# The later modulation units of a mixer-and-FFN kernel, put behind other weight tiles and in another order

## The chip, the cores and the metric

The kernel runs on one core of one Trainium2 chip. The metric is the device time of one execution in microseconds. All data are fp32; a product that has to be exact to fp32 is made of three passes over a rounded high part and a remainder ("hi" and "lo") of each operand.

## The reference

One block of a transformer with adaptive modulation, on 256 tokens of width 1024:

```
mod = silu(c) @ w_ada + b_ada                  # 6 rows of 1024: sh1 sc1 g1 sh2 sc2 g2
h   = x * (1 + sc1) + sh1
y   = token_mixer(h)                           # attention, retention, two gated projections, w_out
x   = layer_norm(ALPHA * x + g1 * y, ln1_g, ln1_b)
h   = x * (1 + sc2) + sh2
y   = conv_ffn(h)                              # gate and up, a convolution of 3 tokens, gelu, down
x   = layer_norm(ALPHA * x + g2 * y, ln2_g, ln2_b)
```

Each row of `mod` is a product of a 1024 x 1024 part of `w_ada` with one vector. It is not made on TensorE: a unit of the weights is loaded with the output index on the partitions, and VectorE multiplies it with the vector and sums along the row.

## The kernel before

**Stages.** A first stage (`h1`, `x_prod`, `halve`) makes the first two modulation rows, h, and the first part of the input projection. Then comes a list of `main` weight tiles, each 128 x 2048 floats (1 MB), in a fixed order: tiles 0 and 1 for the retention keys, 2 to 5 its values, 6 to 9 its gate, 10 to 15 the two merge gates, 16 and 17 the moba projection (`wpm`), 18 to 21 the retention projection (`wpr`), 22 to 25 `w_out`, 26 and 27 the first up block, and from 28 on the gate, up and down tiles of the FFN. Up to tile 23 a tile is used in two steps, one for each half: step s uses half s. `LN1_AT` = 48 is the first step of tiles 24 and 25.

**The way of a tile.** `load_next` (L1237) takes the next entry of `stream` and starts its DMA on the SyncE queue (`load_raw`, L102) into one of `RAW_BUFS` = 4 raw buffers. The buffers go round, so a load waits until the entry four places ahead in the stream has been read for the last time. `prep_halves` (L1242) takes the loaded tiles half by half. For each half, ScalarE rounds it (`whi`, L1263), always one half ahead, and then VectorE makes the remainder (`wlo`, L1277). After the second half the raw buffer is free and the next load is asked for. TensorE uses both in `mm3` (L115 to L117), three matmuls for each product.

**The later modulation rows.** The rows 2 (scale) and 3 (shift) of the second half of the block and the two gates, 4 and 5, each come in four units of 1 MB (`ada_unit`, L952). A unit is put into `stream` behind a weight tile. When `prep_halves` meets one, it puts its two halves on `chain` and goes on with the next weight tile; after each further half of a weight tile it takes one entry off the chain:

```python
    chain.append((raw, half, fn))                # raw_halves, on meeting a unit
    ...
    if chain:                                    # behind each half's wlo
        raw, k, fn = chain.pop(0)
        fn(raw, k, S["main"])                    # one reduction, L227
        if k == 1:
            load_next()
```

So a unit behind tile m has its two reductions behind halves 2m+1 and 2m+2, and its raw buffer is held until then. After the last unit of a row, L957 adds the bias. For the gates `rows_done` (L961) then writes the row of 1024 to DRAM and reads it back as a broadcast to all partitions (L965, L966), both on the GpSimd queue: 4 KB and 0.5 MB. The first gate's broadcast goes to the buffer R0, which the rotated retention operands had before; it is read in L564, after step 47. Scale and shift are read in `out_start` (L702 to L704), after step 48.

**What sets the order.** The engines' programs are written out by the loop over steps (L1312). In step s, `prep_to` prepares halves up to s + 1 + 4 for steps under 22 and up to s + 1 + 6 from there to step 46. Three times a step a piece of the side work is put in between: attention, retention, the transposes, all of it spread over VectorE, ScalarE and TensorE. At the end of a step that completes a product stand the instructions that empty its banks: L518 (ScalarE, the merge gate, after steps 27 and 31), L525 (VectorE, after steps 33 and 35), L544 and L545 (VectorE, after steps 39 and 43). The products take banks 0, 1 and 2, 3 in turn, so the product of steps 34 and 35 uses the banks that L518 empties after step 31, steps 36 to 39 those of the first L525, and so on. Before steps 42 and 45 the merged result is transposed on TensorE (L536) and split (L92, L93). Each engine works through its own program in order; an instruction that waits holds up all that stand behind it on its engine.

The functions that the diff touches, and what calls them:

Of the kernel before, what the change touches and what calls it, by code (L numbers as in the profile page):

```python
# [46 lines left out]
def mixer_ffn(tc, a, out):  # L47
    nc = tc.nc
    pe, act, dve, sp = nc.tensor, nc.scalar, nc.vector, nc.sync
    cst = tc.tile_pool(name="cst", bufs=1)  # L50
    pools = [cst, tc.tile_pool(name="wts", bufs=1), tc.tile_pool(name="big", bufs=1),
             tc.tile_pool(name="tmp", bufs=2),
             tc.tile_pool(name="ps", bufs=1, space=bass.MemoryType.PSUM),
             tc.tile_pool(name="dram", bufs=1, space=bass.MemoryType.DRAM)]
    with tc.manual_schedule():
        with pools[0] as cst, pools[1] as wts, pools[2] as big, pools[3] as tmp, pools[4] as ps, \
                pools[5] as dram:
            _body(nc, a, out, pe, act, dve, sp, cst, wts, big, tmp, ps, dram)


def _body(nc, a, out, pe, act, dve, sp, cst, wts, big, tmp, ps, dram):
# [890 lines left out]
    def ada_unit(secs, u, done):  # L952

        def fn(raw, k, step):
            ada(raw[:, k * 1024:(k + 1) * 1024], secs, 2 * u + k)
            if u == 3 and k == 1:
                dve.tensor_tensor(mod[:, secs], mod[:, secs], bcol[:, secs], OP.add)  # L957
                later.append((step + 7, done))
        return fn

    def rows_done(sec):  # L961

        g = S["g", sec - 4] = slot(f"R{sec - 4}", [128, 1024])
        row = dram.tile([1, 1024], F32, name=f"row{sec}")
        nc.gpsimd.dma_start(row.rearrange("o (p j) -> (o p) j", p=128), mod[:, sec])  # L965
        nc.gpsimd.dma_start(g, row.to_broadcast([128, 1024]))  # L966
# [256 lines left out]


    extra = {}
    for sec, at in ((2, (9, 10, 11, 12)), (3, (13, 14, 15, 16)), (4, (17, 18, 19, 20)), (5, (38, 41, 44, 47))):
        for u in range(4):
            done = (lambda sec=sec: rows_done(sec)) if sec > 3 else (lambda: None)
            extra.setdefault(at[u], []).append((a["ada2"][sec - 2, u], ada_unit(sec, u, done)))
# [204 lines left out]
```

## Time and profile before

| | |
|---|---|
| time, median of 3 runs | 431.37 us (430.92 to 431.76) |
| profiled execution | 431.65 us, span 429.9 us |
| busy: TensorE, VectorE, ScalarE | 416.4, 370.8, 246.0 us |
| DMA | 105.58 MB, mean 246 GB/s |
| the modulation reductions, L227, from 128 x 1024 | 32 (with the first stage's), 38.9 us |
| loads of units (`in_ada`) | 16 of 1 MB |

Busy times overlap; the matmuls are pipelined, so their single durations add up to more than the time they take. A row of the timeline gives the start in us, the duration, the engine and the line, the operation, output and inputs, and in brackets the idle time of the engine ahead of it and what ended that. `AH`, `AYa` and the like are buffers, `P` is a bank of PSUM, `raw`, `whi` and `wlo` are the three forms of a weight tile.

### The profile page before, as it was taken

Reading aid. Unit: us, or ns where it says so; the run is one execution under the profiler, and the core shown is the slowest. Engines: PE = TensorE matmul, PEld = TensorE weight load, DVE = VectorE, ACT = ScalarE, POOL = GpSimd, SP = SyncE. Lnnn points to the kernel's source line nnn. Section 1 sums busy time; section 2 is a strip of 40 time slices with the busy share of each in tenths; the row PEclk is TensorE's granted clock in tenths of the full one; section 3 lists DMA queues with packets and bytes.
Section 4 is the critical chain, followed back from the end, with each engine's and each line's share of the span. In section 5 each row is a group of like instructions: output and inputs, shape, how many; then the busy total and the mean of one; then the engine's idle time right before and its main releaser. Section 6 shows DMA issues by size and latency. Waiting matters only on the chain.

```text
span 429.9 us, 5794 instructions
## 1 busy us (share of the span) xinstructions
PE 416.4 (97%) x2104; PEld 349.6 (81%) x2104; DVE 370.8 (86%) x613; ACT 246.0 (57%) x397; POOL 14.0 (3%) x26
## 2 busy tenths in 40 slices
PE   8999999999999999699999999999999999999993
PEld 4888888887888887578888899888888888888882
DVE  5979899768969989899878897899999888789976
ACT  4666567688953647355433894664555555455700
POOL 0000000100000000000000000100000000002200
PEclk9999999999999999979999999999999999999998
DMA  8998996754387698989953066885875777450001
GB/s 284 408 409 330 418 417 248 285 179 186 110 304 263 217 355 305 348 348 311 386 191 139 2 240 250 311 290 194 307 274 208 287 292 247 185 196 2 1 24 73
DMA packets 18828, 105.58 MB, mean 246 GB/s; under 512 B 2288, under 2 KB 3568, under 8 KB 8048
## 3 DMA queue, kind: packets, MB, share of 16 engines
q1 hardware_dynamic: 17280, 99.97, 62.1%
q0 software_dynamic: 1376, 4.99, 3.4%
q8 instruction: 16, 0.26, 0.2%
q10 hardware_dynamic: 144, 0.26, 0.2%
q14 instruction: 12, 0.10, 0.1%
HBM read 104.15 MB, written 1.06 MB: 245 GB/s over the span
## 4 chain that ended last, share of the span: by engine, by line
PE 87%; DVE 8%; DMA 3%; issue 1%; ACT 0%; DVEq 0%; ACTq 0%; SPq 0%
PE P L124 15%; PE P L115 14%; PE P L116 14%; PE P L117 14%; PE P L301 13%; PE P L126 8%; DVE junk L227 2%; DVE wlo L1277 2%; DMA raw<-in_wpm 2%; DMA raw<-in_wpr 2%; PE P L688 1%; PE P L690 1%; PE P L691 1%; PE P L993 1%; PE P L1048 1%
## 5 line engine op out<-in xcount | busy, mean ns | idle before, releaser
L1277 DVE TENSOR_TENSOR wlo<-raw,whi 128x1024 fp32r<-128x1024 f32 x118 | 142.0, 1218 | 17.0 <-ACT whi L1263 17.0
L1263 ACT ACTIVATE whi<-raw 128x1024 fp32r<-128x1024 f32 x118 | 122.0, 1055 | 48.5 <-PE P L117 14.4
L115 PE MATMUL P<-whi,AH 128*128 128x512 f32 x160 | 63.4, 397 | 0.0
L117 PE MATMUL P<-whi,AH 128*128 128x512 f32 x160 | 62.3, 390 | 0.0
L116 PE MATMUL P<-wlo,AH 128*128 128x512 f32 x160 | 62.3, 389 | 0.0
L301 PE MATMUL P<-whi,AH 128*128 128x512 f32 x160 | 42.0, 392 | 0.0
L227 DVE CUSTOM_DVE_ANT_0 junk<-raw,srow 128x1024 bf16<-128x1024 f32 x32 | 38.9, 1217 | 0.5 <-DMA raw<-in_ada 0.5
L124 PE MATMUL P<-AYa,whi 128*128 128x512 f32 x144 | 39.2, 393 | 0.0
L124 PE MATMUL P<-AYb,whi 128*128 128x512 f32 x144 | 38.6, 390 | 0.0
L301 PEld LDWEIGHTS P<-whi,AH 128*128 128x128 f32 x160 | 29.8, 188 | 7.2 <-ACT whi L284 0.8
L115 PEld LDWEIGHTS P<-whi,AH 128*128 128x128 f32 x160 | 30.0, 188 | 6.8 <-issue 0.7
L117 PEld LDWEIGHTS P<-whi,AH 128*128 128x128 f32 x160 | 30.0, 188 | 6.4
L116 PEld LDWEIGHTS P<-wlo,AH 128*128 128x128 f32 x160 | 30.1, 188 | 5.9
L465 ACT ACTIVATE A<-P 128x256 f32<-128x256 f32 x36 | 13.7, 381 | 34.5 <-PE P L126 32.6
L124 PEld LDWEIGHTS P<-AYb,whi 128*128 128x128 f32 x144 | 27.0, 188 | 6.0
L284 ACT ACTIVATE whi<-raw 128x512 fp32r<-128x512 f32 (+1 forms) x26 | 20.8, 824 | 17.8 <-DMA raw<-in_strm 16.2
L287 DVE TENSOR_TENSOR wlo<-raw,whi 128x512 fp32r<-128x512 f32 (+1 forms) x26 | 23.7, 936 | 6.0 <-ACT whi L284 5.8
L124 PEld LDWEIGHTS P<-AYa,whi 128*128 128x128 f32 x144 | 25.1, 190 | 3.6
L126 PEld LDWEIGHTS P<-AYa,wlo 128*128 128x128 f32 x144 | 22.0, 189 | 2.8
L301 PE MATMUL P<-wlo,AH 128*128 128x512 f32 x80 | 23.3, 391 | 0.0
L126 PE MATMUL P<-AYb,wlo 128*128 128x256 f32 x144 | 23.1, 283 | 0.0
L126 PE MATMUL P<-AYa,wlo 128*128 128x256 f32 x144 | 22.9, 282 | 0.0
(302 smaller groups left out, 739.3 us busy)
## 6 DMA issues: line engine op xcount, KB each, us to landing
raw<-in_ada SPq DMA_DIRECT2D x16, 1024.0 KB, 4.9
raw<-in_wup SPq DMA_DIRECT2D x11, 1024.0 KB, 4.9
raw<-in_wgate SPq DMA_DIRECT2D x11, 1024.0 KB, 5.5
raw<-in_wdown SPq DMA_DIRECT2D x11, 1024.0 KB, 5.2
raw<-in_winB SPq DMA_DIRECT2D x10, 1024.0 KB, 6.3
raw<-in_strm SPq DMA_DIRECT2D x8, 1024.0 KB, 7.8
raw<-in_strm SPq DMA_DIRECT2D x12, 512.0 KB, 7.4
raw<-in_winGr SPq DMA_DIRECT2D x4, 1024.0 KB, 6.1
```

The source lines that it names most:

```text
L115: pe.matmul(o, lh, rh, start=start, stop=False)
L116: pe.matmul(o, lh, rl, start=False, stop=False)
L117: pe.matmul(o, ll, rh, start=False, stop=stop)
L124: pe.matmul(o, wh[:, k * 128:(k + 1) * 128], x2[k], start=k == 0, stop=False)
L126: pe.matmul(o[:, :256], wl[:, k * 128:(k + 1) * 128], x2[k][:, 0], start=False, stop=k == n - 1)
L227: dve.tensor_tensor_reduce(out=nobody(j if own else None), in0=raw, in1=srow, scale=1.0, scalar=0.0, op0=OP.mult, op1=OP.add, accum_out=mo ...
L284: act.activation(hi[:, o], raw[:, o], AF.Copy)
L287: dve.tensor_tensor(lo[:, o], raw[:, o], f(hi[:, o]), OP.subtract)
L301: pe.matmul(pa[b0 + c // 512 * 2 + t], x[xi][:, j, t * 128:(t + 1) * 128], ws[k][:, c:c + 512], start=first and (xi, k) == (0, 0), stop=la ...
L465: act.activation(t, p[:, 256:], AF.Copy)
L1263: act.activation(hi, src, AF.Copy)
L1277: dve.tensor_tensor(lo, src, f(hi), OP.subtract)
```

## The change

The table that says behind which weight tiles the units of each row stand is altered: the first gate's units come first, then scale, then shift, and the twelve units that stood behind the twelve tiles 9 to 20 now stand behind tiles of 8 to 22, with none behind 10, 15 and 19. The units of row 5 stay. Nothing else is touched.

```diff
-    for sec, at in ((2, (9, 10, 11, 12)), (3, (13, 14, 15, 16)), (4, (17, 18, 19, 20)), (5, (38, 41, 44, 47))):
+    for sec, at in ((4, (8, 9, 11, 12)), (2, (13, 14, 16, 17)), (3, (18, 20, 21, 22)), (5, (38, 41, 44, 47))):
         for u in range(4):
             done = (lambda sec=sec: rows_done(sec)) if sec > 3 else (lambda: None)
             extra.setdefault(at[u], []).append((a["ada2"][sec - 2, u], ada_unit(sec, u, done)))
```

## Prediction

> **What bounds the kernel now.** I read the page first, then the waits of TensorE, then the stage around its one large wait.
>
> ```profile
> span 429.9 us, 5794 instructions
> PE 416.4 (97%) x2104; PEld 349.6 (81%) x2104; DVE 370.8 (86%) x613; ACT 246.0 (57%) x397; POOL 14.0 (3%) x26
> ...
> raw<-in_ada SPq DMA_DIRECT2D x16, 1024.0 KB, 4.9
> ```
>
> TensorE is busy 416.4 of 429.9 us, so a change that leaves the matmuls alone can win only where PE waits or runs slowly. Of the waits of PE by line, one is large:
>
> ```profile
> PE P L115 <- ACT A L518: 4.3, 1, 4.3
> ```
>
> The busy times by windows of 5 us, then PE's own rows in order of time, show where it lies (columns of a window: stretch, its length, busy us of PE, PEld, DVE, ACT, POOL, granted clock, DMA share, GB/s):
>
> ```profile
> 180.00:185.00 5.00, 1.59 (x4) 1.30 (x5) 4.24 (x5) 3.19 (x5) 0.00 (x0) 0.63 0.90 341
> 185.00:190.00 5.00, 5.00 (x17) 4.00 (x16) 4.96 (x10) 3.75 (x6) 0.00 (x0) 0.68 0.94 342
> ```
>
> ```profile
> 178.69 0.39 PE L117 MATMUL P<-whi,A 128*128 128x512 f32 x1
> 183.41 0.80 PE L115 MATMUL P<-whi,A 128*128 128x512 f32 x1 [4.33 <-ACT A L518]
> ...
> 188.23 0.39 PE L117 MATMUL P<-whi,A 128*128 128x512 f32 x1
> ...
> 191.18 0.39 PE L115 MATMUL P<-whi,AYa 128*128 128x512 f32 x1
> ...
> 216.55 1.03 PE L536 MATMUL P<-ident,A 128*128 128x128 f32 x8
> 217.34 0.48 PE L115 MATMUL P<-whi,AH 128*128 128x512 f32 x1
> ```
>
> From 188.23 to 191.18 thirteen matmuls take 2.95 us, 0.227 each, so a step of twelve takes 2.72. Step 34 (first half of the second moba-projection tile, weight tile 17) starts at 183.41; it could have at 178.69 + 0.23 = 178.92. That is 4.49 us. Then eleven matmuls up to 188.23 take 4.82 us in place of 2.49, while the clock granted in their window is 0.68: 2.33 more. **At most 6.8 us can be had here.** Without either, step 36 would start at 191.18 - 6.82 = 184.36.
>
> Who is late: ScalarE's rows, then the issues of the raw weight loads on SP, each 1 MB.
>
> ```profile
> 181.81 1.06 ACT L1263 ACTIVATE whi<-raw 128x1024 fp32r<-128x1024 f32 x1 [3.40 <-DMA raw<-in_wpr]
> 182.78 1.07 ACT L518 ACTIVATE A<-P 128x512 f32<-128x512 f32 x2
> ```
>
> ```profile
> 153.74 0.33 SPq L102 DMA_DIRECT2D raw<-in_ada  x1
> 154.99 0.33 SPq L102 DMA_DIRECT2D raw<-in_wpm  x1
> 161.67 0.33 SPq L102 DMA_DIRECT2D raw<-in_ada  x1
> 163.94 0.33 SPq L102 DMA_DIRECT2D raw<-in_wpm  x1
> 168.16 0.33 SPq L102 DMA_DIRECT2D raw<-in_ada  x1
> 170.09 0.33 SPq L102 DMA_DIRECT2D raw<-in_wpr  x1
> 173.51 0.33 SPq L102 DMA_DIRECT2D raw<-in_ada  x1
> 174.85 0.33 SPq L102 DMA_DIRECT2D raw<-in_wpr  x1
> ```
>
> L518 empties the two banks that step 34 needs, and it stands on ScalarE behind the rounding (whi, L1263) of weight tile 19, which is loaded from 174.85 to 181.8. So PE starts 183.41 - 181.81 = 1.60 us after tile 19 lands. With four raw buffers, load n goes out when item n-4 of the stream is released: tile 19 waits for tile 17's second wlo on VectorE. VectorE's rows:
>
> ```profile
> 128.83 1.21 DVE L1159 TENSOR_TENSOR A<-P,A2a 128x384 f32<-128x384 f32 x2 [3.32 <-PE P L1157]
> ...
> 148.99 0.17 DVE L957 TENSOR_TENSOR mod<-mod,first 128x8 f32<-128x8 f32 x1
> ...
> 162.69 1.23 DVE L1277 TENSOR_TENSOR wlo<-raw,whi 128x1024 fp32r<-128x1024 f32 x1 [0.25 <-ACT whi L1263]
> ...
> 173.60 1.22 DVE L1277 TENSOR_TENSOR wlo<-raw,whi 128x1024 fp32r<-128x1024 f32 x1
> 174.74 1.22 DVE L227 CUSTOM_DVE_ANT_0 junk<-raw,srow 128x1024 bf16<-128x1024 f32 x1
> ...
> 182.90 1.23 DVE L1277 TENSOR_TENSOR wlo<-raw,whi 128x1024 fp32r<-128x1024 f32 x1 [0.76 <-ACT whi L1263]
> ...
> 189.99 1.28 DVE L525 TENSOR_TENSOR A<-P,A 128x512 f32<-128x512 f32 x2
> ...
> 202.83 0.68 DVE L544 TENSOR_TENSOR A<-P,A 128x512 f32<-128x512 f32 x1
> ...
> 209.28 1.29 DVE L93 TENSOR_TENSOR AH<-P,AH 128x512 fp32r<-128x512 f32 x2 [0.30 <-ACT AH L92]
> ...
> 212.67 0.69 DVE L544 TENSOR_TENSOR A<-P,A 128x512 f32<-128x512 f32 x1 [0.97 <-PE P L117]
> ...
> 215.37 2.35 DVE L1277 TENSOR_TENSOR wlo<-raw,whi 128x1024 fp32r<-128x1024 f32 x2
> ```
>
> The wlo of 173.60 (half 35, tile 17) gives 174.85. One wlo or one modulation reduction (L227) costs 174.74 - 173.60 = 1.14 us. From 162.69 (half 31) to there the DVE timeline has no idle gap: VectorE's work sets tile 19's issue. After 182.90 VectorE has none until 209.28, and L525, which frees the banks that step 36 needs, frees the first at 190.6, only 0.6 us ahead of 191.18. So behind the wait a second limit lies close.
>
> **The change, part by part.** Nothing is added or removed: 24 reductions, 12 loads, three small sums (L957), one written row and its broadcast. A unit behind tile m puts its reductions behind halves 2m+1 and 2m+2. Before: halves 19 to 42. After: 17 to 20, 23 to 30, 33 to 38, 41 to 46. Up to half 30 both have done 12; from 32 to 38 the new order has done two fewer (2.28 us of VectorE); at 40 to 42 four fewer; at 46 the same.
>
> *The early start.* Two reductions more at halves 17 and 18, made up at 21 and 22. VectorE then waits 3.32 us for PE before 128.83, which hides the 2.28. Without that cover it would cost 2.28 on VectorE. I take 0.
>
> *Tile 19.* From half 31 to 35 two reductions are gone, so the release of tile 17 moves from 174.74 to 172.46, if tiles 16 and 17 are there; they take the places of the units' loads, 153.74 for 154.99 and 161.67 for 163.94. Tile 19 still has a unit's load 1.15 us ahead of it. How long does it take then? Two rows of loads as second of such a pair, in the answers for single loads:
>
> ```profile
> L102 SPq DMA_DIRECT2D raw<-in_winGr x1: 328/328/328, 122.1 to 122.1; - x1
> ...
> DMA to landing us min/median/max: 6.4/6.4/6.4
> ```
>
> ```profile
> L102 SPq DMA_DIRECT2D raw<-in_wpm x1: 328/328/328, 155.0 to 155.0; - x1
> ...
> DMA to landing us min/median/max: 8.1/8.1/8.1
> ```
>
> Before 155.0 two other loads were under way; at 172.5 it is the pair alone with the end of tile 18, as at 122.1. I take 6.4: landing 172.46 + 6.4 = 178.85, not 181.81. Ends: 8.1 gives 180.6; the 4.9 us from issue to landing, the median of the units' loads in the page's rows above, gives 177.4. Step 34 then starts at 178.85 + 1.6 = 180.45: the wait falls from 4.5 to 1.5 us. I take no slow clock after it.
>
> *The gate's row.* The addition at 148.99 is now the gate's, and the two transfers queued on POOL follow it:
>
> ```profile
> 199.80 0.55 POOL L965 DMA_DIRECT2D row<-mod  x1 [62.28 <-DVE mod L957]
> 204.92 0.54 POOL L966 DMA_DIRECT2D AR<-row  x1 [4.58 <-DMA row<-mod]
> ```
>
> They go to about 149.5 and 154.6, among tiles 15 and 16. Nothing else is queued on POOL behind them that anyone waits for before 215, and the buffer of the row has been free since the rotary transposes. But the broadcast moves 0.5 MB: at the 341 GB/s of 180 to 185, 1.5 us of the queue's time. Ends: 0 if it lies in the gaps, 1.5 if all of it delays tile 15 or 16 and so the chain. I take 0.4, nearer the lower end, since tile 16 has a start of 1.25 us. [...]
>
> *What VectorE lets through.* The wlo of half 38 follows tile 19: from 182.90 to 182.90 - 2.96 = 179.95, a lead of 2.95. Half 39 no longer has a reduction, so L525 comes 4.1 us earlier, 185.9, its first bank free at 186.5. PE would want step 36 at 180.45 + 5.44 = 185.9: a wait of 0.6. The first L544 (202.83) has lost the reductions of halves 39 and 40 ahead of it and gained those of 43 to 45: 202.83 - 2.95 - 2.28 + 3.42 = 201.0. The second L544 pair and its sums end at 215.37; without VectorE's own waits of 0.30 and 0.97, which PE being earlier takes away, 214.1. Half 46 adds one more reduction and 0.1 for L957: 214.1 - 2.95 + 2.28 + 0.1 = 213.5. The eight transposes of L536 take 217.34 - 216.55 = 0.79; the last four need this result, so step 45 multiplies from 213.5 + 0.4 = 213.9, where before it did from 217.34. **Gain 3.4**, while PE alone, from 186.5 + (217.34 - 191.18) = 212.7, would have had 4.7. Later the distance holds: VectorE has waits again, and the scale and shift are read only in the LN1 stage, after the last of these steps.
>
> *The sum.* 3.4 - 0.4 = 3.0 us. The profiled execution took 431.65 us (1.75 around the span), 0.3 above the median 431.37 of the runs. 431.37 - 3.0 = **428.4**; the next profile should show a span of about 426.9.
>
> **The rivals.**
>
> *Early.* Tile 19 lands by 177.3 and step 34 doesn't wait. For it: 4.9 us is the common landing. Against: a unit's load lies 1.15 us ahead. Even so the lead on VectorE is bounded: with half 36 waiting for tile 18 (170.09 - 2.28 + 4.9 = 172.7, rounding 1.05) and four operations after it, half 38 starts at 178.4 at best, a lead of 4.5. Gain 4.9: 426.5.
>
> *Slow clock all the same.* The shorter wait is followed by 2.33 us of slow matmuls. Step 36 at 180.45 + 0.4 + 5.44 + 2.33 = 188.6, step 45 at 214.8: gain 2.5, 428.9. For it: the only drop beside the wait in the rows of before. Against: the gap is a third. [...]
>
> *No change.* Tile 19 lands at 181.8 again: 172.46 + 8.1 + 1.3 of the broadcast. The stall and the slow clock return, and VectorE, without a lead, ends the second L544 at 214.1 + 2.4 = 216.5, just in time for the last transposes at 216.95. 431.4.
>
> *Slower.* The four reductions behind halves 43 to 46 stand ahead of L544, in the stretch where VectorE has no idle time. The place is step 45, the price 1 us for each us that the lead of half 38 falls short, and it decides once half 38's wlo comes later than 182.90 + 0.45. That needs tile 19 to land after 182.2: the broadcast and two loads close together holding up tile 15 or 16 by 1.5 and the pair by more than 8.1. Then PE is late by the same at step 34. For 1.6 us: 433.0. Against: 8.1 is the longest such row.
>
> **How the numbers follow.** Forecast 0.55 (its own range 426.9 to 430.0: tile 19 landing in 5.3 us with nothing charged for the broadcast gains 4.5, in 7.4 us with 1.0 charged 1.4), early 0.12, slow clock 0.05, no change 0.13, slower 0.15. Within 0.2% (0.9 us, about what a measurement here can tell) lies the fourth alone: faster 0.72, same 0.13, slower 0.15. The range leaves a part of the early case out below 425.9 and most of the slower above 431.8.
>
> **What would show it.** PE's wait for L518 at 1 to 2 us near step 34, or gone; the granted clock at 1.00 from 180 to 190; the wpr load of tile 19 issued near 172.5 to 173; small waits of PE, under 1 us each, for L525 and for L545 at the L536 transposes. The row's broadcast near 155 with tile 15 and 16 landing at most 1.5 us late. Wrong would be a wait over 3 us for L518, PE waiting in the early rotary transposes near 118, or a wait over 2 us at L536.

## The result and the profile after

The changed kernel takes 429.59 us (median of 22 runs, 428.21 to 431.45), the kernel before in the same comparison 431.9 (22 runs). The ratio is 0.995, its 95% interval 0.9935 to 0.9964: **2.2 us less (1.6 to 2.8)**, where 3.0 were forecast. The time lies inside the range, and the sign is the forecast one.

The profiled execution of the changed kernel took 430.92 us, 1.3 above its median. So its rows show one of its slower executions, and the steps below are read with that in mind. First TensorE's waits by line, the windows around the large one (columns as before), and ScalarE's two rows:

```profile
PE P L115 <- ACT A L518: 4.4, 1, 4.4
```

```profile
180.00:185.00 5.00, 1.78 (x5) 1.46 (x6) 2.98 (x4) 3.37 (x6) 0.00 (x0) 0.85 0.90 354
185.00:190.00 5.00, 5.00 (x20) 3.99 (x19) 4.96 (x10) 3.46 (x7) 0.00 (x0) 0.80 0.83 270
```

```profile
181.63 1.06 ACT L1263 ACTIVATE whi<-raw 128x1024 fp32r<-128x1024 f32 x1 [4.87 <-DMA raw<-in_wpr]
182.59 1.07 ACT L518 ACTIVATE A<-P 128x512 f32<-128x512 f32 x2
```

The wait for L518 is still there, at 4.4 us. Only the slow stretch behind it shrank: the windows before lacked (1 - 0.63 + 1 - 0.68) x 5 = 3.5 us of clock, these lack 1.8. The loads on SyncE and the answer for the single load of tile 19 say where the forecast lead went:

```profile
153.92 0.33 SPq L102 DMA_DIRECT2D raw<-in_wpm  x1
...
167.55 0.33 SPq L102 DMA_DIRECT2D raw<-in_wpr  x1
171.54 0.33 SPq L102 DMA_DIRECT2D raw<-in_ada  x1
173.11 5.46 SPq L102 DMA_DIRECT2D raw<-in_wpr  x2
```

```profile
L102 SPq DMA_DIRECT2D raw<-in_wpr x1: 328/328/328, 173.1 to 173.1; - x1
...
DMA to landing us min/median/max: 8.4/8.4/8.4
```

Tile 19 goes out at 173.11 in place of 174.85, near the forecast: 172.46, and 0.4 more for the broadcast. But it takes 8.4 us, where 6.4 were taken and 8.1 was the upper end, so it lands at 181.5, hardly earlier than before. VectorE's and GpSimd's rows, and the first transposes of the merged result:

```profile
182.72 1.22 DVE L1277 TENSOR_TENSOR wlo<-raw,whi 128x1024 fp32r<-128x1024 f32 x1 [2.02 <-ACT whi L1263]
...
188.66 1.28 DVE L525 TENSOR_TENSOR A<-P,A 128x512 f32<-128x512 f32 x2
...
203.59 0.68 DVE L544 TENSOR_TENSOR A<-P,A 128x512 f32<-128x512 f32 x1
...
213.32 0.68 DVE L544 TENSOR_TENSOR A<-P,A 128x512 f32<-128x512 f32 x1
```

```profile
149.63 0.55 POOL L965 DMA_DIRECT2D row<-mod  x1 [11.92 <-DVE mod L957]
156.18 0.53 POOL L966 DMA_DIRECT2D AR<-row  x1 [6.00 <-DMA row<-mod]
```

```profile
215.79 1.04 PE L536 MATMUL P<-ident,A 128*128 128x128 f32 x8
```

The lead on half 38 is 182.90 - 182.72 = 0.2 us, not 2.95. Step 45's transposes start 0.8 us earlier than before (216.55), and the span is 0.7 shorter. This execution is nearly the rival called "no change"; the median of 22 is not. What differs from one execution to the next is asked below.

### The profile page after: what moved, and what is told of

Same layout as the page of the kernel before. It is cut to its first block, busy times and chain, and to the rows that moved or that the text cites. A ratio compares the mean times of both kernels' runs of the same rounds, so it can differ in the third digit from the quotient of the medians.

```text
span 429.2 us, 5793 instructions
## 1 busy us (share of the span) xinstructions
PE 415.4 (97%) x2104; PEld 349.2 (81%) x2104; DVE 370.5 (86%) x613; ACT 245.6 (57%) x397; POOL 14.0 (3%) x26
## 4 chain that ended last, share of the span: by engine, by line
PE 86%; DVE 6%; DMA 5%; ACT 1%; issue 0%; DVEq 0%; ACTq 0%
PE P L124 15%; PE P L115 14%; PE P L116 14%; PE P L117 14%; PE P L301 13%; PE P L126 8%; DMA raw<-in_wpr 2%; DMA raw<-in_winGr 2%; DVE wlo L1277 2%; DMA raw<-in_wpm 2%; DVE junk L227 1%; ACT whi L1263 1%; PE P L688 1%; PE P L690 1%; PE P L691 1%; PE P L993 1%
```

## The experiments

Each was timed against the kernel before on its own chip, with 4 to 12 runs of each kernel. "Less" is the ratio's distance from 1, times about 432 us; what one kernel has less than another is read from these ratios.

| kernel | median us | ratio to before, 95% interval | less, us |
|---|---|---|---|
| gaps_only | 428.73 | 0.9916 (0.9900 to 0.9931) | 3.6 |
| gate_first_only | 433.32 | 1.0012 (1.0000 to 1.0024) | -0.5 |
| after_l518_first | 431.69 | 0.9984 (0.9970 to 0.9999) | 0.7 |
| after_near36 | 431.69 | 0.9982 (0.9970 to 0.9995) | 0.8 |
| after_again (the changed kernel) | 430.14 | 0.9938 (0.9917 to 0.9959) | 2.7 |
| after_late_row | 428.55 | 0.9906 (0.9881 to 0.9932) | 4.1 |
| spread10 | 426.46 | 0.9849 (0.9824 to 0.9874) | 6.5 |
| no_units | 424.45 | 0.9800 (0.9774 to 0.9825) | 8.7 |
| spread10_gate_first | 426.59 | 0.9864 (0.9851 to 0.9878) | 5.9 |
| loads_only | 424.98 | 0.9827 (0.9813 to 0.9841) | 7.5 |
| reductions_only | 424.47 | 0.9815 (0.9801 to 0.9829) | 8.0 |

The first four shared a chip, then the next four, then the last three.

### The two parts of the change

The theory was that the gaps win, because two reductions fewer lie ahead of tile 17's release, and that the early gate costs something. Against it stood the order of the rows as the cause. First the gaps alone, as an edit of the changed kernel:

```diff
-    for sec, at in ((4, (8, 9, 11, 12)), (2, (13, 14, 16, 17)), (3, (18, 20, 21, 22)), (5, (38, 41, 44, 47))):
+    for sec, at in ((2, (8, 9, 11, 12)), (3, (13, 14, 16, 17)), (4, (18, 20, 21, 22)), (5, (38, 41, 44, 47))):
-                later.append((step + 7, done))
+                later.append((step + (5 if secs == 4 else 7), done))
```

> The new places (8, 9, 11, 12, 13, 14, 16, 17, 18, 20, 21, 22), with the rows in the old order: scale, shift, gate. The gate's row is put out two steps earlier in the program so that it is there at step 47. Theory (fewer reductions ahead of tile 17's release do it, and the gate's broadcast among the loads of tiles 15 and 16 costs some): the kernel before less 2.3 to 3.5 us, that is 0 to 1.2 faster than the changed kernel, as the 0.5 MB now moves after 205. Rival (the order of the rows does it): the time of before. Second rival (the late broadcast comes too late for the first L564): slower than before by 1 us or more, with a wait ahead of L564.

Measured: 3.6 us less than before, just above the 2.3 to 3.5 that the theory said. PE's waits in its profile:

```profile
PE P L115 <- ACT A L518: 2.1, 1, 2.1
...
PE P L536 <- DVE A L545: 0.7, 1, 0.7
PE P L115 <- DVE A L525: 0.5, 1, 0.5
```

These are the three waits of the prediction: the shortened one for L518, and the two small ones where VectorE lets PE go on. No wait for the late broadcast appears. Then the order of the rows alone, as an edit of the kernel before:

```diff
-    for sec, at in ((2, (9, 10, 11, 12)), (3, (13, 14, 15, 16)), (4, (17, 18, 19, 20)), (5, (38, 41, 44, 47))):
+    for sec, at in ((4, (9, 10, 11, 12)), (2, (13, 14, 15, 16)), (3, (17, 18, 19, 20)), (5, (38, 41, 44, 47))):
```

> The old places 9 to 20, with the new order of the rows: gate, scale, shift. Theory: nothing is won, and the broadcast near 155 costs 0 to 1.5 us: the time of before plus 0.4. Rival (the order of the rows does it): before less 2.3 us.

Measured: 0.5 us more than before (0 to 1.0). PE waits for L518 twice:

```profile
PE P L115 <- ACT A L518: 5.6, 2, 4.4
```

So the gaps carry the whole gain, and the order of the rows, if anything, takes some of it back.

### The broadcast by itself

The changed kernel again, and beside it the same kernel with the gate's last addition, and so its row, put behind the first L544 pair:

```diff
-                dve.tensor_tensor(mod[:, secs], mod[:, secs], bcol[:, secs], OP.add)
-                later.append((step + 7, done))
+                add = lambda: dve.tensor_tensor(mod[:, secs], mod[:, secs], bcol[:, secs], OP.add)
+                later.append((step + 17, lambda: (add(), done())) if secs == 4 else (step + 7, (add(), done)[1]))
```

> The changed kernel, unaltered, beside the other three on one chip. Its first profile had tile 19's load take 8.5 us, and PE waiting 4.4 us for L518, where 6.4 and 1.5 to 1.9 were forecast. Theory (that landing varies from one execution to the next and the loads of the units and the broadcast keep it long): 6.4 to 8.5 us again, PE's wait 1.5 to 4.4 us, the time of before less 1.5 to 3. Rival (the landing is fixed by the order of the loads): 8.5 us again to within 0.3.

> The changed kernel with the same places and the same order of the rows, and the same loads; only the gate's last addition (L957), and with it the written row and the broadcast behind it, is put after the first L544 pair, near 205 in place of 149. Theory (the broadcast among the loads of tiles 15 to 19 costs about 1.5 us, as the run with the gate last suggests): 1 to 1.8 us faster than the changed kernel, tile 19 landing 1 to 2 us earlier. Rival (the gate's place in the order matters in some other way, or the earlier difference was one of chips): the time of the changed kernel.

Measured: 430.14 and 428.55 us, 1.4 us apart by the ratios; the two intervals overlap a little. The difference has the sign and size of gaps_only against the changed kernel, and gate_first_only has the same sign in the old places, with an interval that begins at 0. So three comparisons say that the broadcast costs about 0.5 to 1.4 us; none of them settles it by itself. In single loads it is seen at tile 17, asked for at nearly the same moment in both; first the changed kernel, then the late row:

```profile
L102 SPq DMA_DIRECT2D raw<-in_wpm x1: 328/328/328, 161.4 to 161.4; - x1
...
DMA to landing us min/median/max: 6.5/6.5/6.5
```

```profile
L102 SPq DMA_DIRECT2D raw<-in_wpm x1: 328/328/328, 161.2 to 161.2; - x1
...
DMA to landing us min/median/max: 4.8/4.8/4.8
```

With the broadcast of 156.18 in the queue, tile 17 took 1.7 us longer. The rounding of its first half starts 6.6 us after the issue in the changed kernel and 5.2 in the late row; after_again (6.9 us) and gaps_only (5.2) agree. Without it tile 19 goes out at 171.93 in the late row, not at 173.11, where 172.46 was worked out for the case without a broadcast:

```profile
171.93 4.32 SPq L102 DMA_DIRECT2D raw<-in_wpr  x2
```

It then lands in 7.1 us, and PE waits 2.2. A wait of 0.6 us at L536 ends with the moved addition itself, so this edit has a small price of its own:

```profile
PE P L115 <- ACT A L518: 2.2, 1, 2.2
```

In the second profile of the changed kernel the load took 6.7 us, from 173.8, and PE waited 3.6:

```profile
PE P L115 <- ACT A L518: 3.6, 1, 3.6
```

```profile
L102 SPq DMA_DIRECT2D raw<-in_wpr x1: 328/328/328, 173.8 to 173.8; - x1
...
DMA to landing us min/median/max: 6.7/6.7/6.7
```

So the same load in the same kernel took 8.4 and 6.7 us: the rival with a fixed landing falls. Whether this one landing makes the spread of the 22 runs (3.2 us) is not shown by two profiles, and the kernel before spreads by as much (4.3 us).

### Is the wait for L518 all there is?

Two ways to take L518 out from behind tile 19. In the first, ScalarE alone doesn't round ahead in step 31:

```diff
-            ahead = first() if live[0] + 2 <= HL_BUFS else None
+            ahead = first() if live[0] + 2 <= HL_BUFS and S["main"] != 31 else None
```

> The changed kernel; only in step 31 ScalarE no longer rounds one half ahead, so the second L518 stands ahead of the rounding of tile 19 and not behind it. Theory (VectorE is a second limit right behind the first): PE's wait of 4.4 us for L518 goes, and PE then waits 3 to 5 us for the first L525 ahead of step 36, which stands behind half 38's wlo; the time is that of the changed kernel less 0 to 1 us. Rival (the wait for L518 is all there is): the wait and its slow clock go and nothing takes their place, 4.5 to 6 us less than the changed kernel.

Measured: 0.7 us less than before, worse than the changed kernel. The wait for L518 is gone and this one stands in its place, behind VectorE's row:

```profile
PE P L115 <- DVE A L525: 5.3, 1, 5.3
```

```profile
188.06 0.69 DVE L525 TENSOR_TENSOR A<-P,A 128x512 f32<-128x512 f32 x1
```

The mechanism of the theory is confirmed: the next limit is L525, two steps on. Its size was missed: the wait came out 5.3 us, and the kernel is 1.5 us slower than the changed one, not 0 to 1 faster. In the second, four halves of lookahead in place of six, so that ScalarE and VectorE both do the emptying first:

```diff
-LOOKAHEAD, NEAR, NEAR_TO = 6, 4, 22
+LOOKAHEAD, NEAR, NEAR_TO = 6, 4, 36
```

> The changed kernel; the programs prepare only 4 halves ahead, not 6, in steps 22 to 35, so L518, the splits and L525 stand ahead of the work that waits for tile 19 on ScalarE and on VectorE both. Theory: no wait for L518 and none over 1 us for L525; VectorE's amount of work then binds at the first L544, which stands behind halves 43 to 45 (a wait of 1 to 3 us ahead of step 42); before less 3.5 to 5 us, 1.2 to 2.7 faster than the changed kernel. Rival (the DMA's bytes bind, wherever the instructions stand): PE waits for the weights of tile 19 instead, and the time is that of the changed kernel.

Measured: 0.8 us less than before, where 3.5 to 5 were expected. No wait for L518 or L525 is left. But the third place of the prediction takes it all:

```profile
PE P L536 <- DVE A L545: 4.3, 2, 3.6
```

```profile
202.08 0.69 DVE L544 TENSOR_TENSOR A<-P,A 128x512 f32<-128x512 f32 x1
```

So in both kernels the other order of the engines only moved the place where PE waits. The rival of weights arriving late for PE itself is out too: no wait of PE for a rounded or remainder tile of 19 appears.

### VectorE, the loads, or both?

The rows' whole cost, then each half of it. First without the units:

```diff
-    for sec, at in ((4, (8, 9, 11, 12)), (2, (13, 14, 16, 17)), (3, (18, 20, 21, 22)), (5, (38, 41, 44, 47))):
+    for sec, at in ((5, (38, 41, 44, 47)),):
...
-    stream = []
+    [dve.tensor_scalar(mod[:, sec], bcol[:, sec], 0.0, None, op0=OP.add) for sec in (2, 3, 4)]; later.append((29, lambda: rows_done(4))); stream = []
```

> The changed kernel without the three rows: their twelve loads and 24 reductions are left out and the rows hold the bias alone; the gate's row is still written and broadcast. It shows how much the rows cost in all. Theory (PE's one wait and its slow clock are all they cost): before less 6.8 us, and no wait of PE over 0.5 us between 100 and 230. Rival (the rows cost elsewhere too, through the memory or the DMA): more than 8 us less. Second rival (the wait has another cause): less than 5.

Measured: 8.7 us less (7.6 to 9.8), over the 6.8 that I counted at the one place; its profiled execution has no wait of PE in the stage, as the theory said. The rival that the rows cost elsewhere too is not excluded: its mark of 8 lies inside the interval. Then the loads without the reductions, and the reductions without the loads:

```diff
-            ada(raw[:, k * 1024:(k + 1) * 1024], secs, 2 * u + k)
+            ada(raw[:, k * 1024:(k + 1) * 1024], secs, 2 * u + k) if secs == 5 else dve.tensor_scalar(mod[:, secs, 2 * u + k:2 * u + k + 1], raw[:, k * 1024:k * 1024 + 1], 1.0, None, op0=OP.mult)
```

> The changed kernel with its twelve loads of units and its broadcast, but each of the 24 reductions is replaced by a copy of one column (about 0.1 us), so the three rows are not computed. Theory (VectorE's 24 x 1.14 us are what makes tile 19 late and L544 late; the bytes are only a second thing): no wait of PE over 1 us, before less 6.5 to 8, near the kernel without the units. Rival (the bytes of the loads and of the broadcast bind): PE's wait for L518 stays at 2 us or more, before less 1 to 4.

```diff
-            ada(raw[:, k * 1024:(k + 1) * 1024], secs, 2 * u + k)
+            ada(raw[:, k * 1024:(k + 1) * 1024] if secs == 5 else srow, secs, 2 * u + k)
...
-            loaded.append((load_raw(src), fn))
+            loaded.append((load_raw(src) if src is not None else None, fn))
...
-            extra.setdefault(at[u], []).append((a["ada2"][sec - 2, u], ada_unit(sec, u, done)))
+            extra.setdefault(at[u], []).append((a["ada2"][sec - 2, u] if sec == 5 else None, ada_unit(sec, u, done)))
```

> The changed kernel with its 24 reductions, which read a row that is there already, and without the twelve loads; the three rows come out wrong. Theory (VectorE binds at L525 and at the two L544 pairs): tile 19 lands in 5 us and PE's wait for L518 goes, but PE waits for L525 or at the L536 transposes, 1 to 3 us together; before less 4 to 6. Rival (the loads bind): no wait of PE over 0.5 us, before less 7 to 8.7.

Measured: 7.5 us less than before with the loads alone, and 8.0 with the reductions alone, against 8.7 with neither. So each half alone costs about 1 us. The loads alone did what the theory said. For the reductions alone my theory was wrong: it said that VectorE's amount of work would hold PE at L525 and L536 for 1 to 3 us, and no such wait is there. The window from 160 to 210 us of five kernels, in the order changed kernel, spread10 (below), reductions alone, loads alone, no units; the third number is VectorE's busy time, then the DMA's share stands ahead of the GB/s:

```profile
160.00:210.00 50.00, 45.57 (x207) 37.56 (x206) 45.10 (x65) 28.30 (x40) 0.00 (x0) 0.97 0.87 322
```

```profile
160.00:210.00 50.00, 49.84 (x233) 41.29 (x232) 48.02 (x67) 31.00 (x42) 1.08 (x2) 1.00 0.87 333
```

```profile
160.00:210.00 50.00, 50.00 (x236) 41.64 (x234) 49.79 (x72) 28.71 (x39) 0.00 (x0) 1.00 0.56 198
```

```profile
160.00:210.00 50.00, 50.00 (x238) 41.78 (x236) 37.25 (x57) 28.14 (x39) 0.00 (x0) 1.00 0.93 357
```

```profile
160.00:210.00 50.00, 50.00 (x239) 41.82 (x238) 32.68 (x36) 24.48 (x31) 0.00 (x0) 1.00 0.54 191
```

With the reductions alone VectorE works 49.79 of 50 us and is in time for everything: L525 and the first L544 stand 6.1 us earlier than in the changed kernel.

```profile
182.58 0.68 DVE L525 TENSOR_TENSOR A<-P,A 128x512 f32<-128x512 f32 x1
...
197.51 0.69 DVE L544 TENSOR_TENSOR A<-P,A 128x512 f32<-128x512 f32 x1
```

With the loads alone the DMA carries 357 GB/s, more than in the changed kernel, and no wait of PE appears. In the changed kernel VectorE is busy 45.10 us: it is idle for 4.9 us of a stretch in which its work comes too late, 2.02 of them ahead of half 38, for tile 19. So neither the reductions nor the loads are the limit alone. **It is the two together, in a loop:** VectorE stands idle for a load that could go out only when VectorE had released the buffer four places ahead.

One thing stays open. The kernel with the reductions alone leaves out the units' bytes and also their places among the four raw buffers. There tile 19 goes out when tile 15 is released, about 10.5 us earlier than in the changed kernel:

```profile
L102 SPq DMA_DIRECT2D raw<-in_wpr x1: 328/328/328, 162.6 to 162.6; - x1
```

Whether the bytes or the places are what the reductions must meet was not separated. A kernel with the units in a buffer of their own would tell; none was run.

### A version that gives VectorE its idle time back

The unit behind tile 17 goes behind tile 10, into the wait ahead of 129, and the gate stands last but one:

```diff
-    for sec, at in ((4, (8, 9, 11, 12)), (2, (13, 14, 16, 17)), (3, (18, 20, 21, 22)), (5, (38, 41, 44, 47))):
+    for sec, at in ((2, (8, 9, 10, 11)), (3, (12, 13, 14, 22)), (4, (16, 18, 20, 21)), (5, (38, 41, 44, 47))):
```

> Places 8 to 14, 16, 18 and 20 to 22: the unit behind tile 17 goes behind tile 10, so its two reductions lie in VectorE's wait of 3.4 us ahead of 129, and tile 19's load no longer waits for tile 17 but for the unit behind 16. Scale behind 8 to 11, shift behind 12, 13, 14 and 22, the gate behind 16, 18, 20 and 21, so its row moves near 200 to 210. Theory (VectorE's work from half 31 to the second L544 binds): 2.3 us less of it, tile 19 landing 1.5 us or more earlier; before less 4.5 to 6 us, 1 to 2.3 faster than the kernel with the gaps alone, and PE's waits for L518, L525 and L545 under 2 us together. Rival (the landing of the loads binds, whatever VectorE has): the time of the kernel with the gaps alone, before less 3.6.

Measured: **426.46 us, 6.5 less than before (5.4 to 7.6)**, the fastest of the kernels that compute everything; the theory said 4.5 to 6. PE's only wait in the stage, tile 19's load and its rounding:

```profile
PE P L536 <- DVE A L545: 0.6, 2, 0.5
```

```profile
L102 SPq DMA_DIRECT2D raw<-in_wpr x1: 327/327/327, 171.8 to 171.8; - x1
...
DMA to landing us min/median/max: 4.8/4.8/4.8
```

```profile
176.70 1.06 ACT L1263 ACTIVATE whi<-raw 128x1024 fp32r<-128x1024 f32 x1 [3.65 <-PE P L1198]
177.66 1.07 ACT L518 ACTIVATE A<-P 128x512 f32<-128x512 f32 x2
```

Tile 19 goes out about as early as in after_late_row, but with no unit 1.15 us ahead of it, and lands in 4.8 us in place of 7.1. L518 comes before 179.2, when PE wants its banks. The rival's time, 3.6 less than before, is excluded. Its mechanism is not: the gain over after_late_row is 2.4 us, and the landing is 2.3 us shorter. VectorE has 2.28 us less to do ahead of L544 as well, and no run changes one without the other. Its four runs lie within 0.6 us (426.17 to 426.72), the 22 of the changed kernel within 3.2. The same places with the gate first:

```diff
-    for sec, at in ((2, (8, 9, 10, 11)), (3, (12, 13, 14, 22)), (4, (16, 18, 20, 21)), (5, (38, 41, 44, 47))):
+    for sec, at in ((4, (8, 9, 10, 11)), (2, (12, 13, 14, 16)), (3, (18, 20, 21, 22)), (5, (38, 41, 44, 47))):
```

> The places 8 to 14, 16, 18, 20 to 22, but with the order of the changed kernel, so the gate's broadcast goes out near 146 to 152, among the loads of tiles 14 to 16. Theory (the broadcast costs what it delays tiles 15 to 19, and less where VectorE has a lead of 2 us): 0.5 to 1.5 us slower than the same places with the gate last, that is before less 5 to 6. Rival (with the lead it is hidden): the same time, before less 6.5.

Measured: 5.9 us less than before, 0.6 from spread10 with intervals that overlap: undecided between the theory and the rival. The broadcast has also moved, to a time with less traffic (in the changed kernel 138 GB/s from 145 to 150 us, 364 from 155 to 160):

```profile
145.20 0.54 POOL L966 DMA_DIRECT2D AR<-row  x1 [4.88 <-DMA row<-mod]
```

Against the changed kernel, whose order of rows it has, this is one unit moved from 17 to 10 and the broadcast 11 us earlier.

## Why the prediction was right or wrong

The number lies inside the range, and what carries the gain is the part of the mechanism that was forecast: gaps_only has it without the new order of the rows. But the picture drawn for the changed kernel was not seen in it. Both of its profiles have a wait over 3 us for L518 (4.4 and 3.6), which the prediction named as a sign of being wrong, and a granted clock of 0.80 to 0.85 where 1.00 was forecast. The wait of about 2 us and the small waits behind it appear in the two kernels without the early broadcast. So it is in part luck that the time came out within 1.2 us of the forecast.

- **What bounds the kernel:** right. L518 behind the rounding of tile 19 is the one large wait; the gaps shorten it (2.1 us in gaps_only, 2.2 in after_late_row). The ceiling of 6.8 us was low: without the units it is 8.7 (7.6 to 9.8).
- **The early start at 0:** right. No profile of the changed kernel has a wait of PE between 100 and 178.
- **Tile 19, the issue:** nearly right. 172.46 was worked out without the broadcast, 171.93 and 172.79 were measured in after_late_row and gaps_only; with its 0.4 it is 172.9, and 173.1 and 173.8 were measured.
- **Tile 19, the landing, taken as 6.4 us:** mis-sized. It took 8.4 and 6.7 us in two profiles, 7.1 and 6.8 without the broadcast; the upper end of 8.1 was passed. The nearest row was this load itself before the change, also second behind a unit: the prediction's own times, 174.85 and 181.8, make it about 6.9 us.
- **No slow clock after the wait:** wrong for most executions, as far as the record shows. The clock fell in both profiles of the changed kernel (0.80 to 0.85) and in that of after_late_row (0.66 from 180 to 185). Of the 22 runs, 13 have a mean granted clock of 0.992 or less, so they lack 3.2 us of clock or more. The end of the program accounts for 1.4 us of that in the trace of before and 1.7 in that of the changed kernel; spread10, with 1.00 from 100 to 230, lacks 2.5 us in all (0.994 of 424.4). That a gap of 1.5 us leaves the clock at 1.00 was my estimate: no profiled execution of the changed kernel had so short a wait. The wait of 2.06 us in gaps_only left it at 1.00, the one of 2.22 in after_late_row did not.
- **The gate's row, taken as 0.4 us:** mis-sized. It is 0.5 to 1.4 by three comparisons. This term, the landing and the clock all make the gain smaller than 3.0; how the missing 0.8 us is shared among them isn't shown. Tile 17 took 6.5 us with the broadcast in the queue, 4.8 without (after and after_late_row). The prediction's upper end of 1.5 would have given a gain of 1.9 us, nearer to 2.2 than my 3.0. That its time, 429.5, lies next to the measured 429.59 is partly luck, since the kernel before took 431.9 in the comparison and not 431.37.
- **What VectorE lets through:** the working holds where its order is unchanged. For a lead x of half 38 it puts the first L544 at 202.83 - x + 1.14. With x = 0.18 that is 203.8, and 203.59 was measured. The later place of the reductions, behind 41 to 46, costs what was said. Wrong is the reading behind it, that VectorE's work is a limit of its own: reductions_only shows that it isn't one without the loads.
- **The rivals:** the first profile is nearly "no change" (4.4 us, tile 19 landing at 181.5). "Slow clock all the same" is what after_again and after_late_row show: a shorter wait (3.6 and 2.2 us), and behind it matmuls at a lower granted clock (0.85 and 0.66 from 180 to 185). "Early" was not seen in the changed kernel, but is what spread10 does. "Slower" was not seen.

## What to carry to other kernels

Where a few buffers pass from loads to an engine and back, the busy shares of that engine and of the DMA may not show the limit: here VectorE was busy 45.10 of 50 us, the DMA's share was 0.87, and neither was the limit alone. Take each half away alone; if both times fall to nearly the same floor, the two limit each other, and one way to open the loop is to move work to where the engine waits for something else. A stall on one engine is only the first of a row of deadlines; before one is removed, work out from the order of instructions which one comes next, since here two ways of removing the wait moved it by two and by eight steps and won less than the change did. A small transfer on another queue was not free here, where loads were what was late: 0.5 MB cost 0.5 to 1.4 us.

## What the runs showed of the hardware

The clock fell after a wait much shorter than the 4.49 us of before: PE waited 2.22 us in after_late_row and 2.06 in gaps_only, at the same place, and it fell in the first alone (0.66 from 180 to 185, against 1.00). In the trace of before, half rate lasts 6.83 us (181.34 to 188.17) and comes again at 427.10, behind the last matmul; in that of the changed kernel it lasts 3.41 us (183.54 to 186.96) and comes again at 425.89. From the end of the first to the second it is 238.93 us in both, so in these two traces the changes lie 2, 1 and 70 times 3.413 us apart. The windows below keep to such steps; first two of after_late_row, then two of gaps_only (the second number is PE's busy time, the one ahead of the DMA's share is the clock):

```profile
177.18:180.59 3.41, 1.34 (x6) 0.76 (x5) 1.55 (x4) 1.44 (x3) 0.00 (x0) 1.00 0.92 315
180.59:184.01 3.42, 3.27 (x8) 2.62 (x9) 3.38 (x6) 3.42 (x8) 0.00 (x0) 0.50 0.84 333
```

```profile
177.71:181.12 3.41, 1.56 (x7) 0.94 (x5) 1.81 (x4) 1.39 (x2) 0.00 (x0) 1.00 1.00 401
181.12:184.54 3.42, 3.21 (x14) 2.68 (x15) 3.38 (x6) 3.42 (x8) 0.00 (x0) 1.00 0.83 323
```

In after_late_row PE is idle for 3.41 - 1.34 = 2.07 us of one window, and the next is granted at half rate. In gaps_only it is idle for 1.85 us of one window, the rest of the wait falls into the next, and the clock stays. In the window that ends where the half rate begins, PE is idle for 2.26 us in before (177.93 to 181.34) and for 3.09 in the changed kernel (180.13 to 183.54). So in these four profiles the clock fell behind windows with 2.07 us or more of idle PE, and stayed behind one with 1.85. How it would go in other executions isn't shown.

The 1.7 us of clock lacking in after_late_row fits one such window at 0.50, the 3.5 of before two.

The load of tile 19 (1 MB), asked for 1.1 to 1.6 us behind a unit's, took 6.7 (after_again) to 8.4 us (the first profile of the changed kernel) in eight profiles. In the two of the spread10 kernels, where the unit's goes out 3.4 us ahead of it, it took 4.8. In the changed kernel it differed by 1.7 us between two executions.
